# Moving the small transfers of a blocked inverse from SP's queue to ACT's in a hybrid decoder layer

## The chip, the cores and the metric

The kernel runs on one core of a Trainium2 chip. A core has a matrix engine (TensorE, here PE, with its weight loads shown apart as PEld), a vector engine (VectorE, DVE), a scalar engine (ScalarE, ACT), a general engine (GpSimd, POOL) and a queue engine (SyncE, SP). Each works through its own instructions in order and meets the others at semaphores. DMAs are issued from the queues of SP, ACT and POOL. The matrix engine writes to PSUM, the other operands lie in SBUF, and what doesn't fit goes through DRAM.

The metric is the device time of one execution in microseconds, as a median over runs.

## The reference

One layer of a decoder trunk on x of shape (1, 1024, 2048), all in float32, followed by an RMSNorm:

```python
h = rmsnorm(x, ln_g)
proj = h @ w_in                       # 2048 -> 6672 columns, split among three groups
out_a = gmlp_spatial_gating(...) * silu(g_z)          # 4 groups x 128, chunks of 128
out_b = rmsnorm(gated_delta_rule(q, k, v, g, beta)) * silu(d_z)   # 8 heads of 128
out_c = softmax(cq @ mk.T / sqrt(128)) @ mv * silu(c_z)           # 4 heads, 256 memory tokens
y = rmsnorm(x + concat(out_a, out_b, out_c) @ w_out, final_g)
```

The part that the change touches is in the gated delta rule. For each head and chunk it needs the inverse of a unit lower triangular matrix:

```python
a = where(strict, (k * beta) @ k.T * decay, 0)
T = triangular_solve(a + eye, eye, lower=True, unit_diagonal=True)
value, k_cumdecay = T @ (v * beta), T @ (k * beta * exp(g_cum))
```

## The kernel before

**Products.** Each large float32 product is made of three passes over operands split into a rounded high part and a rest (`split_to`, `triple`): ACT casts the high part, DVE subtracts for the low one, PE runs high-high, high-low and low-high. The first half of the heads is projected directly, in two halves of 512 tokens. The other projections and the output projection go through a scheme of seven products for eight (`seven`, `blocks`), whose sums of blocks are formed on DVE and kept in DRAM (`s_d`). A product's result gathers in one of four PSUM banks `acc`; the smaller products of the heads use four banks `dn`.

**The delta rule.** The kernel works on chunks of 128 tokens and on two heads at a time (a pair), in halves of 512 tokens: four chunks x two heads give eight 128 x 128 triangles per pair and half, in one tile `gt`. `front` makes q, k and `gt`. The inverse of a triangle is built from its four 32 x 32 diagonal blocks:

- `blocks_out` (line 967) stores the diagonal blocks to DRAM tensors `gdr`, one DMA for each of the four block positions. A DMA moves rows of 32 numbers (128 bytes).
- `inverse` (980) loads them so that every block lies in one partition (32 partitions per `gdr`, 1024 numbers in each; four loads per `gdr`), and runs 31 steps of two DVE instructions on all blocks at once, with a copy that transposes at the end. Two stores per `gdr` put the inverted blocks and their transposes into DRAM tensors `tdr` and `udr`.
- `levels` (1008) loads them back into block positions of the tiles `tblk` and `ut` (twelve loads and one transfer within `gt`), joins blocks of 32 to 64 and of 64 to 128 with small float32 products, and ACT copies the results out of PSUM.
- `scan_step` (1079) then carries the heads' states through the four chunks.

The first two pairs are inverted one at a time, for each half: four calls of `inverse`, on one `gdr` each. The last two pairs of both halves are gathered (`gdrs`) and inverted by one call on four `gdr` tensors, named "late", whose results are used by four later `levels` calls.

**The order of the work.** No instruction is placed by hand. Every call goes through `Engine` to `Plan.add`, which records it with its dependences. `Plan.price` gives it an estimated duration, and `Plan.issue` replays the whole program with these estimates: each engine takes, among what is ready, the lowest rank (`rank(...)`, 5 if none is given) and then the oldest. The order found is what each engine gets; at run time only semaphores hold an instruction back, so an engine waits at the first instruction whose data isn't there.

In that replay a DMA costs its issuing queue 380 ns on SP, 100 ns on ACT and 800 ns on POOL, less the engine's overlap (`OVERLAP`: none on SP, on ACT 90 ns but at most half the cost). The bytes of all DMAs push one cursor, `dma`, at 300 bytes per ns; a transfer lands 1600 ns after its end on the cursor, plus 3000 ns for a store to DRAM or 2400 ns for a load of small pieces. A product on PE costs 13.3 ns plus its columns at 2.4 per ns times its passes, at least 110 ns, and 30 ns if it doesn't fill 128 partitions.

`V`, `S`, `G`, `PE` and `Q` in the code are DVE, ACT, POOL, PE and the queue of SP. Nearly all DMAs are issued from `Q`: weights, block sums, spills and the inverse's transfers share it. Beside it ACT issues five small loads at the start and four stores at the very end. All instructions go out from line 277 (`o.fn(*o.args, **o.kw)` in `Plan.issue`), so the profile shows that line for everything, and tiles tell the groups apart.

Of the kernel before, what the change touches and what calls it, by code (L numbers as in the profile page):

```python
# [17 lines left out]
P = 128  # L18
# [44 lines left out]
class Plan:  # L63
# [21 lines left out]
    @contextmanager  # L85
    def rank(self, cls):
        old, self.cls = self.cls, cls
        yield
        self.cls = old
# [91 lines left out]
    def price(self, o, name, outs, ins):  # L181

        out = outs[0]
        n = math.prod(out.shape[1:])
        both = [*outs, *ins]
        psum = any(i.space == PSUM for i in both)
        pointer = any(i.shape[-1] == 1 and math.prod(i.shape[1:]) == 1 for i in ins[1:])
        o.nbytes = o.lock = 0
        o.lat = 0.0
        if name == "dma_start":  # L190
            o.cost = {"sp": 380.0, "act": 100.0, "pool": 800.0}[o.eng]
            rows = math.prod(out.shape[:-1])
            o.nbytes = max(4 * math.prod(out.shape), 512 * rows)
            src = ins[0]
            pieces = src.shape[-1] < 128 or out.shape[-1] < 128
            if out.space == DRAM:
                o.lat = 3000.0
            elif pieces or out.shape[0] < 32:
                o.lat = 2400.0
            elif list(src.ap)[0][0] == 0:  # L200
                o.lat = 4000.0
        elif o.eng == "pe":
            passes = 1 if ins[0].dtype == F32R else 2 if name == "transpose" else 4
            o.cost = max(13.3 + n / 2.4 * passes, 110.0) if out.shape[0] == P else 30.0
            o.lat = 175.0
        elif o.eng == "act":
            o.cost = (165.0 if psum else 200.0) + 0.82 * n + (105.0 if pointer else 0.0)
            o.cost += 190.0 if "accum_out" in o.kw else 0.0
        elif o.eng == "dve":
            n = max([n] + [math.prod(i.shape[1:]) for i in ins])  # L210
            o.cost = (n + 151) / 0.96 + (60.0 if pointer and name == "scalar_tensor_tensor" else 0.0)
            o.lock = not psum and (name.startswith("tensor_") or name == "scalar_tensor_tensor")
            o.lock = o.lock and name != "tensor_reduce"
        else:
            o.lock = 1
            if name in ("memset", "affine_select"):
                o.cost = 100.0 + 0.83 * n * (1 if name == "memset" else 1.4)
                o.lat = 800.0 if name == "affine_select" else 0.0
            else:
                o.cost = 750.0 + 150.0 * (n - 1) if n < 8 else 200.0 + 2.1 * n  # L220

    def issue(self):
        free = dict.fromkeys(self.SEEN, 0.0)
        soon = {e: [] for e in free}
        now = {e: [] for e in free}
        held = {"dve": 0.0, "pool": 0.0}
        dma = 0.0
        for o in self.ops:
            if o.n == 0 and o.lead is o:
                heapq.heappush(soon[o.eng], (0.0, o.idx))  # L230
        left = len(self.ops)
        while left:
            best = None
            for e in free:
                if now[e]:
                    t = free[e]
                elif soon[e]:
                    t = max(free[e], soon[e][0][0])
                else:
                    continue  # L240
                if best is None or t < best[0]:
                    best = (t, e)
            t, e = best
            while soon[e] and soon[e][0][0] <= t:
                i = heapq.heappop(soon[e])[1]
                heapq.heappush(now[e], (self.ops[i].cls, i))
            head = self.ops[heapq.heappop(now[e])[1]]
            for o in (head, *head.tail):
                t = max(t, free[e])
                o.at = t  # L250
                left -= 1
                if o.lock:
                    t = max(t, held["pool" if e == "dve" else "dve"])
                end = t + o.cost
                if o.lock:
                    held[e] = end
                free[e] = end - min(self.OVERLAP[e], 0.5 * o.cost)
                done = end + o.lat
                if o.nbytes:
                    dma = max(dma, end) + o.nbytes / self.DMA_RATE  # L260
                    done = dma + self.DMA_FIXED + o.lat
                for s in o.succ:
                    if s.eng != e or o.nbytes:
                        when = done + self.SEEN[s.eng] + (self.SLACK if s.eng == "pe" else 0.0)
                    elif e == "pe":
                        when = free[e]
                    else:
                        when = end + 34.0
                    s.ready = max(s.ready, when)
                    s.n -= 1  # L270
                    if s.n == 0:
                        heapq.heappush(soon[s.eng], (s.ready, s.idx))
            if len(head.tail) > 7:
                free[e] += self.SWITCH
        self.ops.sort(key=lambda o: (o.at, o.idx))
        for o in self.ops:
            o.fn(*o.args, **o.kw)  # L277
# [3 lines left out]
def kernel(  # L281
# [21 lines left out]
    x, mem, w_in, out = x[0], mem[0], w_in[0], out[0]  # L303
# [7 lines left out]
    V, S, G, PE, Q = R.dve, R.act, R.pool, R.pe, R.sp  # L311
# [5 lines left out]
    def DT(shape, name, dt=F32):  # L317
        return dr.tile(list(shape), dt, name=name, tag=name)[:]
# [35 lines left out]
    def bc(ap, n):  # L354
        return ap.unsqueeze(ap.ndim).to_broadcast(list(ap.shape) + [n])

    def rep(ap, n):
        return ap.unsqueeze(1).to_broadcast([ap.shape[0], n, ap.shape[1]])
# [211 lines left out]
    for k in range(KT):  # L570
# [11 lines left out]
        for h in range(NX):  # L582
            sl = slice(h * P, (h + 1) * P)
            triple(ka[h][:, :NMEM], (hi[:, sl], lo[:, sl]), (mh[:, kk], ml[:, kk]), k == 0, k == KT - 1)
        for mt in range(2):
            sl = slice(mt * P, (mt + 1) * P)
# [104 lines left out]
    for g in range(NG):  # L691
        sl = slice(g * P, (g + 1) * P)
# [274 lines left out]
    def blocks_out(gt, n):  # L967

        gv = gt.rearrange("p h t i -> p (h t) i")
        gdr = [DT([8, 32, 32], f"gdr{n}_{b}") for b in range(4)]  # L970
        for b in range(4):
            sl = slice(b * 32, (b + 1) * 32)
            with rank(1):
                Q.dma_start(gdr[b].rearrange("c j i -> j c i"), gv[sl, :, sl])
        return gdr

    def flat(start, *aps):
        start(*(a.rearrange("p a b -> p (a b)") for a in aps))

    def inverse(gdrs, n, cls):  # L980

        nr = 32 * len(gdrs)
        gd = ring["inv"]()[0:nr].rearrange("p (a b) -> p a b", b=32)
        for i, gdr in enumerate(gdrs):
            for b in range(4):
                with rank(1):
                    flat(Q.dma_start, gd[i * 32 + b * 8 : i * 32 + (b + 1) * 8], gdr[b])
        ti = ring["inv"]()[0:nr].rearrange("p (a b) -> p a b", b=32)
        tmp = (y1 if nr == 32 else y2)[0:nr].rearrange("p c m -> p (c m)")
        with rank(4):  # L990
            G.memset(ti, 0.0)
            G.affine_select(out=ti, in_=ti, compare_op=ALU.not_equal, fill=1.0, base=0,
                            pattern=[[1, 32], [-1, 32]], channel_multiplier=0)
        with rank(cls):
            for j in range(31):
                n1, m = 31 - j, j + 1
                tv = tmp[:, 0 : n1 * m].rearrange("p (n m) -> p n m", m=m)
                V.tensor_tensor(out=tv, in0=bc(gd[:, j, j + 1 :], m), in1=rep(ti[:, j, 0:m], n1), op=ALU.mult)
                V.tensor_tensor(out=ti[:, j + 1 :, 0:m], in0=ti[:, j + 1 :, 0:m], in1=tv, op=ALU.add)
            V.tensor_copy(gd.rearrange("p i m -> p m i"), ti)  # L1000
        tdr, udr = ([DT([32, 32, 32], f"{t}{n}_{i}") for i in range(len(gdrs))] for t in ("tdr", "udr"))
        for i in range(len(gdrs)):
            with rank(1):
                flat(Q.dma_start, tdr[i], ti[i * 32 : (i + 1) * 32])
                flat(Q.dma_start, udr[i], gd[i * 32 : (i + 1) * 32])
        return list(zip(tdr, udr))

    def levels(gt, tdr, udr):
# [179 lines left out]
    def inverted(n, *states):  # L1188
        return [(*s[:-1], i) for s, i in zip(states, inverse([s[-1] for s in states], n, 3))]
# [324 lines left out]
    with rank(2.6):  # L1514
        late_inv = inverse(gdrs, "late", 1.9)
# [265 lines left out]
```

## Time and profile before

| | before |
|---|---|
| median of 3 runs | 1648.26 us (1644.93 to 1648.33) |
| the profiled execution | 1647.33 us |
| its span, first to last instruction | 1645.6 us |
| mean granted clock of PE | 0.997 |
| busy PE / PEld | 1615.4 / 1354.1 us |
| busy DVE / ACT / POOL | 1323.4 / 1025.8 / 117.1 us |
| share of the span with DMA engines busy, SP's queue | 77.7% |
| bytes moved | 419.51 MB, 255 GB/s |

A busy time is the time in which the engine had an instruction at work. Issuing a DMA isn't counted as busy; the timeline shows it apart, with a q behind the engine's name (SPq, ACTq). Matmuls are pipelined and overlap in the records: a 128 x 512 product lasts 390 to 395 ns there, while the next one starts 0.23 us after it. An idle time in brackets stands in front of the instruction that ended it, with the engine or transfer that was waited for. A name such as `inv<-gdr` is the output tile and the input, without buffer numbers: here the loads of `inverse`. A float32 product that isn't split leaves two records on PE.

The profile shows the inverse's transfers as `gdr<-gt` (stores of `blocks_out`), `inv<-gdr`, `tdr<-inv` and `udr<-inv` (and `tdrlate`, `udrlate` for the late group), then `tblk<-tdr` and `ut<-udr` in `levels`.

### The profile page before, as it was taken

What the parts mean: (1) busy time and instruction counts of PE and PEld (TensorE: products, weight loads), DVE (VectorE), ACT (ScalarE), POOL (GpSimd) and SP (SyncE); (2) the same over time, 40 slices, a digit from 0 to 9 for tenths busy, and PEclk for the clock granted to TensorE, in tenths of its full rate; (3) what the DMA queues carried; (4) which work ended last, traced back from release to release, by engine and by line L of the source; (5) the groups of instructions that cost most, each with busy time, mean ns of one, the idle gap of its engine ahead of it and who ended that gap; (6) DMA issues with size and microseconds to landing.
All of it is one profiled execution on the core that took longest, in us unless ns stands there. A gap on an engine that the chain in (4) does not pass through costs nothing.

```text
span 1645.6 us, 26195 instructions
## 1 busy us (share of the span) xinstructions
PE 1615.4 (98%) x8570; PEld 1354.1 (82%) x8570; DVE 1323.4 (80%) x2288; ACT 1025.8 (62%) x2235; POOL 117.1 (7%) x139
## 2 busy tenths in 40 slices
PE   8999999899999999999999999999999999999997
PEld 6888887788888888888888787888888888888886
DVE  4866796767879869899999898879678898688875
ACT  6957764576846446877686546766657774344445
POOL 0001110210200000100101101000000000000001
PEclk9999999999999999999999999999999999999999
DMA  8989888586887877579877887889778789678646
GB/s 265 257 233 278 261 275 258 178 247 200 265 287 238 265 236 231 183 266 331 303 229 243 293 277 208 276 281 303 249 240 279 258 281 352 200 269 300 220 143 241
DMA packets 316659, 419.51 MB, mean 255 GB/s; under 512 B 57773, under 2 KB 138342, under 8 KB 316522
## 3 DMA queue, kind: packets, MB, share of 16 engines
q1 hardware_dynamic: 314818, 414.67, 77.7%
q0 software_dynamic: 1088, 2.10, 0.5%
q8 instruction: 67, 1.10, 0.3%
q10 hardware_dynamic: 616, 1.07, 0.2%
q14 instruction: 70, 0.57, 0.1%
HBM read 334.33 MB, written 82.87 MB: 254 GB/s over the span
## 4 chain that ended last, share of the span: by engine, by line
PE 88%; DVE 4%; DMA 4%; issue 1%; ACT 1%; POOL 1%; SPq 0%; POOLq 0%; DVEq 0%; ACTq 0%
PE acc L277 67%; PE dn L277 21%; DMA wraw<-in_w_in_dram 1%; DVE alo L277 1%; DVE wlo L277 1%; DVE y L277 1%; DMA wraw<-hTd 1%; POOL hs L277 1%; DMA E<-gcd 0%; DMA sd<-zg 0%; ACT whi L277 0%; DVE kT L277 0%; DMA y<-in_w_in_dram 0%; SPq L277 0%; DMA el<-vd 0%
## 5 line engine op out<-in xcount | busy, mean ns | idle before, releaser
L277 PE MATMUL acc<-ahi,whi 128*128 128x512 f32 (+1 forms) x1152 | 453.0, 394 | 7.3 <-ACT xr L277 4.5
L277 PE MATMUL acc<-ahi,wlo 128*128 128x512 f32 (+1 forms) x1152 | 451.1, 392 | 0.4 <-DVE small L277 0.4
L277 PE MATMUL acc<-alo,whi 128*128 128x512 f32 (+1 forms) x1152 | 450.6, 391 | 0.0
L277 PEld LDWEIGHTS acc<-ahi,whi 128*128 128x128 f32 x1152 | 217.3, 189 | 49.7 <-ACT xr L277 5.2
L277 PEld LDWEIGHTS acc<-ahi,wlo 128*128 128x128 f32 x1152 | 217.3, 189 | 41.7 <-DVE small L277 0.6
L277 PEld LDWEIGHTS acc<-alo,whi 128*128 128x128 f32 x1152 | 217.4, 189 | 40.7
L277 PE MATMUL acc<-ahi,zh 128*128 128x512 f32 x736 | 234.6, 395 | 0.9 <-DVE gt L277 0.9
L277 ACT CAST whi<-wraw 128x512 fp32r<-128x512 f32 (+1 forms) x170 | 137.1, 808 | 105.6 <-PE acc L277 67.1
L277 DVE TENSOR_TENSOR alo<-raws,ahi 128x1024 fp32r<-128x1024 f32 x131 | 159.9, 1221 | 38.6 <-ACT ahi L277 37.3
L277 ACT CAST ahi<-raws 128x1024 fp32r<-128x1024 f32 x131 | 137.4, 1049 | 69.1 <-PE dn L277 28.2
L277 DVE TENSOR_TENSOR wlo<-wraw,whi 128x1024 fp32r<-128x1024 f32 (+1 forms) x138 | 134.4, 975 | 49.1 <-ACT whi L277 43.1
L277 PEld LDWEIGHTS acc<-ahi,zh 128*128 128x128 f32 x736 | 137.2, 188 | 27.9 <-DVE gt L277 1.1
L277 PE MATMUL acc<-ahi,zl 128*128 128x512 f32 x368 | 145.1, 394 | 0.0
L277 DVE TENSOR_TENSOR ahi<-y,ahi 128x1024 fp32r<-128x1024 f32 x65 | 79.3, 1220 | 20.5 <-ACT ahi L277 20.2
L277 ACT CAST ahi<-y 128x1024 fp32r<-128x1024 f32 x65 | 68.2, 1049 | 39.4 <-PE acc L277 21.8
L277 PEld LDWEIGHTS acc<-ahi,zl 128*128 128x128 f32 x368 | 69.3, 188 | 13.1
L277 POOL TENSOR_TENSOR hs<-hs,mhalf 128x4 f32<-128x4 f32 x32 | 54.7, 1711 | 229.8 <-DVE hs L277 223.3
L277 ACT CAST zh<-wraw 128x1024 fp32r<-128x1024 f32 x36 | 37.8, 1051 | 44.4 <-PE acc L277 27.6
L277 POOL TENSOR_TENSOR small<-small,mhalf 128x1 f32<-128x1 f32 x26 | 19.6, 757 | 577.1 <-DVE small L277 577.1
L277 PE MATMUL dn<-whi,alo 128*128 128x512 f32 x152 | 59.1, 390 | 0.0
L277 PE MATMUL dn<-wlo,ahi 128*128 128x512 f32 x152 | 59.0, 389 | 0.0
L277 PE MATMUL dn<-whi,ahi 128*128 128x512 f32 x152 | 58.9, 390 | 0.0
(397 smaller groups left out, 3201.5 us busy)
## 6 DMA issues: line engine op xcount, KB each, us to landing
wraw<-in_w_in_dram SPq DMA_DIRECT2D x268, 256.0 KB
raws<-sd SPq DMA_DIRECT2D x148, 256.0 KB
y<-in_w_in_dram SPq DMA_DIRECT2D x92, 256.0 KB
y<-sd SPq DMA_DIRECT2D x77, 256.0 KB
wraw<-in_w_out_dram SPq DMA_DIRECT2D x64, 256.0 KB
raws<-h0d SPq DMA_DIRECT2D x54, 256.0 KB
y<-in_w_out_dram SPq DMA_DIRECT2D x33, 256.0 KB
low<-wlo SPq DMA_DIRECT2D x32, 256.0 KB
```

Source lines behind the costliest of these rows:

```text
L277: o.fn(*o.args, **o.kw)
```

## The change

Three things change. The stores of `blocks_out`, the loads of `inverse` and the stores at its end are issued from ACT's queue (`S`) and no more from SP's (`Q`). The loads of `levels` stay on SP. In the replay, a DMA of ACT has a cursor of its own, `beside`, on which its bytes count double, and it doesn't push the cursor of the other DMAs. And the estimate of an unsplit float32 product (four passes) that fills 128 partitions is at least 222 ns, where 110 was the floor for all.

```diff
@@ Plan.price
         elif o.eng == "pe":
             passes = 1 if ins[0].dtype == F32R else 2 if name == "transpose" else 4
-            o.cost = max(13.3 + n / 2.4 * passes, 110.0) if out.shape[0] == P else 30.0
+            o.cost = max(13.3 + n / 2.4 * passes, 222.0 if passes == 4 else 110.0) if out.shape[0] == P else 30.0
             o.lat = 175.0
@@ Plan.issue
-        dma = 0.0
+        dma = beside = 0.0
...
                 done = end + o.lat
-                if o.nbytes:
+                if o.nbytes and e == "act":
+                    beside = max(beside, end) + 2 * o.nbytes / self.DMA_RATE
+                    done = beside + self.DMA_FIXED + o.lat
+                elif o.nbytes:
                     dma = max(dma, end) + o.nbytes / self.DMA_RATE
                     done = dma + self.DMA_FIXED + o.lat
@@ blocks_out
-                Q.dma_start(gdr[b].rearrange("c j i -> j c i"), gv[sl, :, sl])
+                S.dma_start(gdr[b].rearrange("c j i -> j c i"), gv[sl, :, sl])
@@ inverse
-                    flat(Q.dma_start, gd[i * 32 + b * 8 : i * 32 + (b + 1) * 8], gdr[b])
+                    flat(S.dma_start, gd[i * 32 + b * 8 : i * 32 + (b + 1) * 8], gdr[b])
...
-                flat(Q.dma_start, tdr[i], ti[i * 32 : (i + 1) * 32])
-                flat(Q.dma_start, udr[i], gd[i * 32 : (i + 1) * 32])
+                flat(S.dma_start, tdr[i], ti[i * 32 : (i + 1) * 32])
+                flat(S.dma_start, udr[i], gd[i * 32 : (i + 1) * 32])
```

The lines that move stand under `rank(1)`, the lowest rank in use here, as before. Among 128 x 128 and wider products the new floor changes nothing (13.3 + 128 / 2.4 x 4 is already 226.6); it acts on the products of 64 columns in `levels` and on two of 32 columns in each `decays`.

## The prediction

> **What bounds the kernel now.** I read the page's engine totals first, then the busy time by stage, then every idle stretch of PE, then the transfers that move. The totals:
>
> ```profile
> span 1645.6 us, 26195 instructions
> PE 1615.4 (98%) x8570; PEld 1354.1 (82%) x8570; DVE 1323.4 (80%) x2288; ACT 1025.8 (62%) x2235; POOL 117.1 (7%) x139
> ```
>
> PE is busy for 1615.4 of 1645.6 us. No schedule can take more than the 30.2 us left, and no product is added or removed. The table by stage shows where those are (columns: stage, its width, busy time of PE, PEld, DVE, ACT, POOL, granted clock, DMA share, GB/s):
>
> ```profile
> 0.00:100.00 100.00, 92.54 (x569) 79.48 (x570) 65.78 (x124) 72.07 (x148) 6.45 (x18) 1.00 0.87 265
> 100.00:185.00 85.00, 85.00 (x431) 71.49 (x430) 58.50 (x112) 60.70 (x159) 11.04 (x15) 1.00 0.85 252
> 185.00:320.00 135.00, 129.96 (x715) 108.36 (x713) 106.36 (x268) 79.14 (x230) 14.03 (x10) 0.99 0.80 248
> 320.00:480.00 160.00, 156.63 (x960) 132.07 (x958) 120.02 (x255) 109.03 (x299) 26.60 (x24) 1.00 0.76 242
> 480.00:620.00 140.00, 140.00 (x751) 117.46 (x750) 110.43 (x185) 71.05 (x133) 3.23 (x5) 1.00 0.76 242
> 620.00:920.00 300.00, 295.71 (x1394) 245.67 (x1393) 277.66 (x441) 219.13 (x474) 29.57 (x33) 1.00 0.77 256
> 1020.00:1180.00 160.00, 158.31 (x1091) 135.91 (x1091) 129.79 (x200) 106.15 (x246) 8.68 (x14) 1.00 0.84 274
> ```
>
> The first 100 us come before any moved transfer. Between 185 and 1180 us PE idles 5.04 + 3.37 + 4.29 + 1.69 = 14.4 us; the rest is the start and the final drain. So the stage that holds the inverses has 14.4 us to win. The timeline of PE names the stretches; these rows carry most of them (in brackets the idle time and what ended it):
>
> ```profile
> 253.33 0.51 PE L277 MATMUL acc<-ahi,whi 128*128 128x512 f32 x1 [1.73 <-ACT xr L277]
> 312.72 0.80 PE L277 MATMUL acc<-ahi,whi 128*128 128x512 f32 x1 [2.81 <-ACT xr L277]
> 315.87 0.49 PE L277 MATMUL acc<-alo,whi 128*128 128x512 f32 x1
> 316.43 0.40 PE L277 MATMUL acc<-ahi,whi 128*128 128x512 f32 x1
> 316.66 0.40 PE L277 MATMUL acc<-alo,whi 128*128 128x512 f32 x1
> 324.15 1.21 PE L277 MATMUL dn<-ident,vs 128*128 128x128 f32 x4 [1.64 <-ACT vs L277]
> 381.69 0.49 PE L277 MATMUL dn<-states,kT 128*128 128x128 f32 x2 [0.82 <-ACT vs L277]
> 906.35 0.44 PE L277 MATMUL dn<-ident,gt 128*128 128x128 f32 x2 [1.39 <-ACT E L277]
> 1022.95 1.16 PE L277 MATMUL dn<-wsT,el 128*128 128x128 f32 x8 [1.69 <-DMA el<-vd]
> ```
>
> Five of these six end with a late ACT, one with a late transfer. None ends directly with an inverse's transfer. After the stall at 312.72 PE is also slow: from 312.72 to 315.87 seven products take 3.15 us from start to start, 0.45 each, where two of the same kind a little later (316.43 and 316.66) start 0.23 apart. That is about 1.5 us more, with the mean granted clock of that stage at 0.99.
>
> **The change, part by part.**
>
> *What moves.* Eighty DMA issues go from SP's queue to ACT's: 32 stores in `blocks_out`, 32 loads in `inverse`, 16 stores at its end. The transfers themselves, the loads of `levels` and all arithmetic stay. Each costs its queue this (minimum, median, maximum, ns):
>
> ```profile
> L277 SPq DMA_DIRECT2D gdr<-gt x32: 303/448/2274, 187.1 to 907.0; - x32
> L277 SPq DMA_DIRECT2D inv<-gdr x32: 263/293/588, 195.2 to 913.1; - x32
> L277 SPq DMA_DIRECT2D tdr<-inv x4: 318/408/442, 263.5 to 566.5; - x4
> L277 SPq DMA_DIRECT2D udr<-inv x4: 318/438/511, 264.6 to 569.7; - x4
> 995.11 2.73 SPq L277 DMA_DIRECT2D tdrlate<-inv  x4
> 997.94 1.77 SPq L277 DMA_DIRECT2D udrlate<-inv  x4
> ```
>
> 32 x 0.448 + 32 x 0.293 + 4 x 0.408 + 4 x 0.438 + 2.73 + 1.77 = 31.6 us of issuing leave SP. SP isn't the bound; its relief counts only where PE waits behind it.
>
> The Trainium skill, DMA: Bandwidth & Descriptors, section Issuing engines are not separate DMA queues, speaks against the change: DMAs run on the same engines whoever issues them, and issuing from several saves only the issuing time, usually small beside the transfer. By that rule the two gains that I find next would be nothing, and the sum below -1.2 instead of -3.7 us.
>
> *The late group's stores.* That is so once:
>
> ```profile
> 1000.72 2.85 SPq L277 DMA_DIRECT2D tblk<-tdrlate  x6
> 1003.61 8.16 SPq L277 DMA_DIRECT2D ut<-udrlate  x12
> 1011.87 0.38 SPq L277 DMA_DIRECT2D vd<-E  x1
> 1017.85 0.43 SPq L277 DMA_DIRECT2D el<-vd  x1
> ```
>
> From 995.11 to 999.71 SP issues eight inverse stores, then eighteen loads of `levels`, and only at 1011.87 the store whose reload ends the 1.69 us stall. Without the stores the eighteen loads can start up to 4.5 us sooner, as their source lands. I take the whole 1.69 us; the ends are 0 (the loads still wait for the landing) and 1.69. Behind it nothing else is late: the next product follows in that row's group.
>
> *The inverse loads of the third early pair.*
>
> ```profile
> 361.57 4.52 SPq L277 DMA_DIRECT2D gdr<-gt  x4
> 373.27 2.16 SPq L277 DMA_DIRECT2D inv<-gdr  x3
> 376.02 0.34 SPq L277 DMA_DIRECT2D wlo<-low  x1
> 376.61 0.26 SPq L277 DMA_DIRECT2D inv<-gdr  x1
> 380.91 0.18 DVE L277 TENSOR_TENSOR y<-inv,inv 32x31 f32<-32x31 f32 x1 [1.94 <-DMA inv<-gdr]
> ```
>
> The fourth load stands behind a weight load. DVE then stops 1.94 us for it with the state update queued behind, ACT's `vs` copy waits for that, and PE loses the 0.82 us at 381.69. Issued straight after the third (375.43) it would land 1.2 us sooner. That covers the 0.82; ends 0 and 0.82.
>
> *ACT's side.* The only ACT issues at steady work stand at the end:
>
> ```profile
> 1636.44 0.41 ACTq L277 DMA_DIRECT2D out_dram<-vs  x1
> 1637.05 0.46 ACTq L277 DMA_DIRECT2D out_dram<-y  x1
> ```
>
> So an issue on ACT costs about what it does on SP, and the first of a burst can run beside ACT's current instruction (1636.44 lies inside the activation of 1636.31 to 1637.01). ACT gets some 31.6 us on top of 1025.8, 3%, and is idle 620 us. The cover is that idle time. Without it a burst of four stores puts 4 x 0.448 = 1.8 us ahead of casts and PSUM copies. The loads' wait for the stores' landing now stands in ACT's queue; between the first store's and the first load's issue at 361.57 and 373.27 lie 11.7 us, so I count no wait there. The planner charges an ACT issue 100 ns less an overlap of 50, so it sees 4 us of the 31.6. The five stalls above that end with ACT sum to 8.4 us; 3% of that is 0.3 us, my term. The ends: 0, and 10 us if a third of the unplanned 27.6 us reaches PE (the rival below).
>
> *Estimates of small products.* Sixty-four products of `levels` go from 120 ns (13.3 + 64/2.4 x 4) to 222 in the plan, and four of `decays` from 110. The trace:
>
> ```profile
> 1015.86 1.00 PE L277 MATMUL dn<-tblk,gt 128*128 128x64 f32 x8
> 1016.67 0.71 PE L277 MATMUL acc<-ahi,zh 128*128 128x512 f32 x2
> ```
>
> Eight records are four fp32 products (two records each: the 64 products leave 128): 0.81 us, 202 ns each. The plan was 0.33 us short per group, 0.66 per `levels`, and will be 0.16 long. Stalls within some 40 us behind a `levels` call and not counted yet are 2.81 + 1.64 us and the 1.5 of slow clock, 6.0 us. I take a quarter, 1.5 us, as an estimate; ends are the whole 6.0 gained and, since the planner draws every order after the first `decays` anew, as much lost.
>
> *The model's DMA cursor.* ACT's transfers no longer push the cursor of SP's loads, and count double on their own. That changes order alone; it is in the ends just given.
>
> *Sum.* -1.69 - 0.82 + 0.3 - 1.5 = -3.7 us. The profiled execution took 1647.33 us (1.7 outside the span): 1643.6. The median of the runs, 1648.26, lies 0.9 above it, so 1644.5 beside the median. A measurement here tells 0.2%, 3.3 us, from no change; the forecast lies just beyond.
>
> **The rivals.**
>
> *ACT becomes the late one (slower).* ACT runs in order, so a store waiting for `gt`, or 1.8 us of issuing, delays the casts and copies behind it. Worst places are the four gdr stores at 361.57, 4.52 us in SP, while ACT would be copying for `levels`; and the eight stores at 995, where ACT empties PSUM:
>
> ```profile
> 996.12 0.58 ACT L277 COPY y<-acc 128x512 f32<-128x512 f32 x1
> 1000.19 0.58 ACT L277 COPY y<-acc 128x512 f32<-128x512 f32 x1
> ```
>
> Those four copies free the banks of the next product. For it: five of six stalls already end with ACT, and the plan is blind to 27.6 us. Against: ACT was idle 38%, and its casts mostly wait for PE to free a buffer (total us, times, longest):
>
> ```profile
> ACT whi L277 <- PE acc L277: 112.9, 90, 5.2
> ```
>
> If a third reaches PE, +9.2 - 2.5 = +6.7: 1655.0. With some nineteen bursts, it decides once 0.2 us of each sticks out (3.7/19), and it is slower by over 0.2% from 0.37 us.
>
> *The new order is worse (slower).* The present order has 14.4 us of stalls; one more like that at 312.72 with its slow clock, 4.3 us, and another like 253.33, 1.73, without the planned gains: 1654.3.
>
> *It is hidden anyway.* No PE gap ends with an inverse's transfer, and the two I count vanish into others, with the estimates' term at half and ACT's cost set against it: 1647.33 + 0.9 + 0.3 - 0.7 = 1647.8.
>
> This is where the rule of the Trainium skill quoted above (DMA: Bandwidth & Descriptors) leads. The trace so far bears it out in that SP's issuing is the one saving it shows.
>
> *More than I count (faster).* The gaps at 253.33, 312.72 with its clock, 324.15, 381.69 and 1022.95 all go: 1.73 + 4.3 + 1.64 + 0.82 + 1.69 = 10.2: 1638.1.
>
> **How the numbers follow.** Forecast 0.36, its own range 1640 to 1646; more gained 0.10; hidden 0.13; late ACT 0.27; worse order 0.14. The forecast's range crosses the bound of 0.2% at 1645.0, so 0.05 of it counts as same, and 0.02 of "hidden" as faster. Faster 0.31 + 0.10 + 0.02 = 0.43, same 0.05 + 0.11 = 0.16, slower 0.27 + 0.14 = 0.41. The range runs from just below the larger gain, 1637, to beyond the late ACT's 1655, 1658.
>
> **What would show it.** Right: the 80 issues stand under ACT's queue; the row at 1022.95 without its 1.69 us and DVE's wait for inv<-gdr gone; PE's idle time between 185 and 1180 at 11 us or less. Late ACT: ACT's time before casts and copies grows and PE's stalls ended by ACT come to more than 8.4 us. Worse order: stalls at new places whose waits name DVE or POOL, with ACT's issues standing in idle stretches. The prediction is wrong if ACT is held by one issue for 2 us (the longest on SP was 2274 ns) at a scan step, or if new stalls each bring the slow clock with them.

## The result, and the profile after

| | before | after |
|---|---|---|
| median of 6 runs each | 1648.96 us (1644.93 to 1655.01) | 1668.7 us (1666.13 to 1674.22) |
| ratio, with its 95% interval | 1 | 1.0118 (1.0092 to 1.0145) |
| the profiled execution, its span | 1647.33, 1645.6 us | 1666.31, 1664.6 us |
| mean granted clock of PE | 0.997 | 0.992 |

The change makes the kernel 1.2% slower. The forecast was 1644.5, the range 1637 to 1658: wrong in sign, and outside the range.

The engine totals of the changed kernel (all its instructions go out from line 280 now):

```profile
span 1664.6 us, 26198 instructions
PE 1623.0 (98%) x8570; PEld 1355.5 (81%) x8570; DVE 1317.2 (79%) x2288; ACT 1023.2 (61%) x2235; POOL 108.1 (6%) x139
```

The span is 19.0 us longer. PE's idle time grows from 30.2 to 41.6 us, its busy time from 1615.4 to 1623.0 with the same 8570 records. So PE stands still more, and is slower for a while. The busy time by stage (columns as in the prediction) says where:

```profile
185.00:320.00 135.00, 131.50 (x727) 109.14 (x726) 110.13 (x280) 83.74 (x249) 10.85 (x11) 1.00 0.81 242
320.00:480.00 160.00, 153.54 (x937) 128.71 (x936) 110.93 (x245) 102.41 (x287) 21.02 (x24) 0.98 0.76 229
480.00:620.00 140.00, 137.92 (x729) 114.88 (x728) 114.73 (x188) 75.11 (x140) 2.04 (x6) 0.99 0.77 254
620.00:920.00 300.00, 290.39 (x1348) 240.09 (x1347) 262.41 (x423) 207.29 (x448) 27.65 (x27) 0.98 0.77 254
920.00:1020.00 100.00, 96.04 (x519) 78.75 (x518) 88.28 (x155) 50.85 (x74) 8.52 (x12) 1.00 0.81 253
1020.00:1180.00 160.00, 160.00 (x1105) 137.52 (x1104) 129.19 (x208) 112.77 (x271) 13.14 (x17) 1.00 0.84 268
```

PE idles 25.6 us in these rows (before: 14.4), more than before in the four from 320 to 1020 us, and the clock falls to 0.98 in two of them. The timeline of PE has the stalls:

```profile
355.80 1.01 PE L280 MATMUL acc<-ident,tn 128*128 128x128 f32 x4 [1.83 <-ACT jk L280]
368.21 0.71 PE L280 MATMUL dn<-vs,ut 128*128 128x128 f32 x4 [2.62 <-ACT ut L280]
491.18 1.21 PE L280 MATMUL dn<-ident,vs 128*128 128x128 f32 x4 [2.08 <-ACT vs L280]
690.76 0.39 PE L280 MATMUL dn<-inv 128*128 128x256 f32 x1 [1.98 <-ACT inv L280]
894.51 0.48 PE L280 MATMUL dn<-ident,gt 128*128 128x128 f32 x1 [5.34 <-ACT gt L280]
898.04 0.48 PE L280 MATMUL dn<-ident,gt 128*128 128x128 f32 x1 [1.78 <-ACT gt L280]
1009.02 1.10 PE L280 MATMUL dn<-ut,y 128*128 128x64 f32 x8 [2.72 <-ACT y L280]
1016.68 1.06 PE L280 MATMUL dn<-wsT,el 128*128 128x128 f32 x8
```

All seven long ones end with ACT. The last row answers the 1.69 us stall of before at 1022.95: that product waits for nothing now. What ACT does ahead of the two stalls near 895 us stands in its own timeline (ACTq are the DMAs that it issues):

```profile
869.94 1.06 ACT L280 CAST ahi<-y 128x1024 fp32r<-128x1024 f32 x1
870.80 7.61 ACTq L280 DMA_DIRECT2D inv<-gdr  x12
878.46 0.40 ACT L280 ACTIVATE E<-E,hs 128x128 f32<-128x128 f32 x1 [7.46 <-DMA inv<-gdr]
...
884.69 3.49 ACTq L280 DMA_DIRECT2D gdr<-gt  x4
888.22 1.05 ACT L280 CAST whi<-wraw 128x1024 fp32r<-128x1024 f32 x1 [5.50 <-issue]
...
893.56 0.27 ACTq L280 DMA_DIRECT2D inv<-gdr  x1
893.87 0.59 ACT L280 COPY gt<-acc 128x512 f32<-128x512 f32 x1 [1.25 <-DMA wraw<-in_w_in_dram]
897.09 0.27 ACTq L280 DMA_DIRECT2D inv<-gdr  x1
897.40 0.59 ACT L280 COPY gt<-acc 128x512 f32<-128x512 f32 x1 [2.95 <-DMA raws<-sd]
```

The two copies of `gt` out of PSUM start as soon as the loads issued at 893.56 and 897.09 let them, and PE's products start 0.64 us after each copy's start. (The transfers in the brackets are those that landed last by the profile. Neither copy reads them; why ACT waits for them is the subject of a section below.) Before that the burst of twelve loads keeps ACT from any work for 7.46 us; twelve issues at their median of 281 ns are 3.4 of that, the rest is waiting between them. The waits of ACT name the inverse's transfers, which before's did not. Two of them:

```profile
ACT E L280 <- DMA inv<-gdr: 7.5, 1, 7.5
ACT kd L280 <- DMA gdr<-gt: 3.4, 1, 3.4
```

The other part of the loss is the clock. Busy time in windows of 2 us, the granted clock third from the end of each row:

```profile
890.00:892.00 2.00, 0.00 (x0) 0.00 (x0) 2.00 (x3) 2.00 (x5) 0.00 (x0) 0.96 0.45 81
892.00:894.00 2.00, 0.00 (x0) 0.00 (x0) 1.70 (x6) 0.75 (x2) 0.00 (x0) 0.50 0.97 337
900.00:902.00 2.00, 2.00 (x7) 1.48 (x6) 0.19 (x1) 1.26 (x2) 0.00 (x0) 0.50 0.94 315
902.00:904.00 2.00, 2.00 (x11) 1.60 (x10) 2.00 (x5) 1.21 (x2) 0.00 (x0) 0.98 0.31 87
```

From 892 to 902 us PE has half its clock, partly while it is idle. Adding (1 - clock) x busy time of PE over windows of 1 us from 100 to 1620 us gives 1.6 us before and 8.0 after. With the idle time between 100 and 1620 us (14.4 and 25.9 us) that is +6.4 and +11.5, 17.9 us of the 19.0 that the span is longer. The table below does the same for each run.

### The profile page after: what moved, and what is told of

Read it like the earlier page. It is cut to its first block, busy times and chain, and to the rows that moved or that the text cites. A ratio compares the mean times of both kernels' runs of the same rounds, so it can differ in the third digit from the quotient of the medians.

```text
span 1664.6 us, 26198 instructions
## 1 busy us (share of the span) xinstructions
PE 1623.0 (98%) x8570; PEld 1355.5 (81%) x8570; DVE 1317.2 (79%) x2288; ACT 1023.2 (61%) x2235; POOL 108.1 (6%) x139
## 4 chain that ended last, share of the span: by engine, by line
PE 72%; DMA 7%; DVE 5%; ACT 2%; issue 2%; ACTq 0%; SPq 0%; POOL 0%; POOLq 0%; DVEq 0%
PE acc L280 54%; PE dn L280 18%; DMA wraw<-in_w_in_dram 1%; DVE alo L280 1%; DMA E<-gcd 1%; DVE y L280 1%; DVE wlo L280 1%; DMA inv<-gdr 1%; DMA y<-in_w_in_dram 1%; ACTq L280 0%; ACT ahi L280 0%; DMA raws<-sd 0%; DVE ai L280 0%; DVE inv L280 0%; DMA zg<-hTd 0%
## 5 line engine op out<-in xcount | busy, mean ns | idle before, releaser
L280 POOL TENSOR_TENSOR hs<-hs,mhalf 128x4 f32<-128x4 f32 x32 | 48.4, 1516 | 204.4 <-DVE hs L280 203.4
L280 ACT CAST whi<-y 128x1024 fp32r<-128x1024 f32 x34 | 35.8, 1052 | 38.8 <-issue 20.4
```

## The experiments

My theory after this result, A: ACT, which works in order, is held by the DMAs in its own stream. The rival, B: the order that the planner draws anew is worse, wherever the DMAs stand. A recorded DMA can be sent from another queue than the planner thinks (its `fn` is replaced after recording), so the order and the queue can be changed one without the other.

| run | order | the eighty DMAs | ratio to before (95%) | PE idle, 100 to 1620 us | lost to half clock, us | span |
|---|---|---|---|---|---|---|
| before | old | SP | 1 | 14.4 | 1.6 | 1645.6 |
| after | new | ACT | 1.0118 (1.0092 to 1.0145) | 25.9 | 8.0 | 1664.6 |
| e1 | 222 ns alone | SP | 1.0033 (1.0016 to 1.0051) | 17.5 | 7.5 | 1654.1 |
| e2 | without 222 ns | ACT | 1.0117 (1.0094 to 1.0140) | 25.8 | 7.7 | 1666.9 |
| e3 | new | SP | 1.0057 (1.0038 to 1.0077) | 19.5 | 6.2 | 1655.4 |
| e4 | old | ACT | 1.0107 (1.0085 to 1.0128) | 25.0 | 6.7 | 1665.9 |
| e5 | old | stores ACT, loads SP | 1.0041 (1.0024 to 1.0059) | 19.7 | 1.5 | 1655.7 |
| e6 | old | loads ACT, stores SP | 1.0040 (1.0023 to 1.0056) | 17.0 | 4.6 | 1650.5 |
| e7 | old | POOL | 0.9991 (0.9976 to 1.0006) | 10.5 | 1.7 | 1643.6 |
| e8 | ACT's DMAs at 650 ns | ACT | 1.0238 (1.0207 to 1.0269) | 36.2 | 14.2 | 1686.7 |
| e9 | old | SP, and 80 spare on ACT | 1.0104 (1.0086 to 1.0122) | 26.5 | 9.2 | 1668.2 |
| e9b | old | SP, and 80 spare on POOL | 1.0007 (0.9993 to 1.0020) | 11.9 | 3.0 | 1648.6 |
| e12 | old | SP, and 160 spare copies on ACT | 1.0027 (1.0011 to 1.0043) | 18.5 | 6.4 | 1655.7 |
| e13 | old | SP, and 80 spare copies on ACT | 1.0021 (1.0005 to 1.0038) | 13.6 | 4.8 | 1650.3 |
| e10 | floor 130 ns | SP | 1.0043 (1.0028 to 1.0059) | 14.3 | 2.6 | 1657.5 |
| e14 | floor 160 ns | SP | 1.0139 (1.0118 to 1.0159) | 19.7 | 3.4 | 1668.6 |
| e11 | planned for POOL | POOL | 1.0018 (1.0003 to 1.0033) | 15.2 | 5.2 | 1651.2 |

The three columns on the right are of one profiled execution each; the idle time is 1520 us less PE's busy time there. For e6 and e7 that execution is a quick one (1652.21 us beside a median of 1657.3, and 1645.28 beside 1649.26), so their columns look better than the ratio.

### Order and queue apart (e1 to e4)

e1 is before with the new floor alone:

```diff
-            o.cost = max(13.3 + n / 2.4 * passes, 110.0) if out.shape[0] == P else 30.0
+            o.cost = max(13.3 + n / 2.4 * passes, 222.0 if passes == 4 else 110.0) if out.shape[0] == P else 30.0
```

> Kernel before with the floor of 222 ns alone; no DMA moves. Theory A (ACT is held by its own DMA issues, which the plan hardly sees): the estimate has no part in the loss, so 0.997 to 1.003 of before, about 1649 us. Theory B (the order drawn anew is worse whatever queue the DMAs stand in): a good part of the 19 us shows here, 1.006 or more.

e2 is the changed kernel with that line as it was.

> Changed kernel with the floor back at 110 ns: the eighty DMAs on ACT and the second cursor alone. Theory A: 1.008 to 1.015 of before, about as slow as the whole change, with ACT again the end of PE's stalls. Theory B (the estimate's new order is at fault): under 1.005.

e3 is the changed kernel, planned as it is, with the eighty DMAs sent from SP; e4 is the kernel before, planned as it is, with them sent from ACT. The edit of e4 (the other four calls alike; in e3 `S` and `nc.sync`):

```diff
-                Q.dma_start(gdr[b].rearrange("c j i -> j c i"), gv[sl, :, sl])
+                Q.dma_start(gdr[b].rearrange("c j i -> j c i"), gv[sl, :, sl]).fn = nc.scalar.dma_start
```

> The changed kernel's order of instructions on every engine, but the eighty DMAs are issued from SP's queue. Theory A: PE's stalls behind ACT at 368, 491 and 890 to 900 us and the half-speed stretches behind them go, and the time returns to 0.997 to 1.004 of before. Theory B: the order stays as bad as it is, 1.008 or more, with the same stalls.

> The order of the kernel before on every engine, but the eighty DMAs are issued from ACT's queue, at the places that they had on SP relative to the rest of the program. Theory A: ACT is held as in the changed kernel, or more since nothing was planned round it: 1.008 to 1.02 of before. Theory B: near 1.000, 0.997 to 1.004, as the order is the old one.

The queue is the larger part. With the old order it costs 1.07%, 17.6 us, on its own (e4). The order costs too: 0.57%, 9.4 us, with every DMA on SP (e3), where theory A had at most 0.4%. Together they cost 1.18%, not the sum. One reason that the traces show is that both make the stretch near 370 to 380 us wait. PE's timeline there in e3,

```profile
371.08 0.79 PE L280 MATMUL dn<-states,kT 128*128 128x128 f32 x2 [4.69 <-DVE states L280]
```

and in e4,

```profile
381.22 1.22 PE L277 MATMUL dn<-states,kT 128*128 128x128 f32 x4 [4.15 <-ACT vs L277]
921.61 0.44 PE L277 MATMUL dn<-ident,gt 128*128 128x128 f32 x2 [3.87 <-ACT E L277]
```

where before had 0.82 and 1.39 us. And in e3 the changed kernel's pair of stalls near 895 us is gone: the same twelve loads, in the same order of the program, leave SP while ACT goes on. SP's rows in e3:

```profile
871.57 0.97 SPq L280 DMA_DIRECT2D inv<-gdr  x3
...
873.04 2.35 SPq L280 DMA_DIRECT2D inv<-gdr  x7
...
875.84 0.66 SPq L280 DMA_DIRECT2D inv<-gdr  x2
```

and ACT's beside them:

```profile
870.72 1.05 ACT L280 CAST ahi<-y 128x1024 fp32r<-128x1024 f32 x1
871.67 0.40 ACT L280 ACTIVATE E<-E,hs 128x128 f32<-128x128 f32 x1
```

The activation of `E` follows its cast at once, where the changed kernel has the 7.46 us. Not every stall behind ACT is the queue's, though. The one of 2.08 us at 491.18 in the changed kernel, which theory A expected to go, stays in e3 with all eighty on SP:

```profile
491.13 1.21 PE L280 MATMUL dn<-ident,vs 128*128 128x128 f32 x4 [2.11 <-ACT vs L280]
```

That one belongs to the order. The estimate alone (e1) is a loss, 0.33%, between the two theories, and without it (e2) the change is as slow as with it.

### Which of the DMAs (e5, e6)

In e5 only the 48 stores have their `fn` replaced, in e6 only the 32 loads.

> The old order; only the 48 stores (gdr, tdr, udr) are issued from ACT, the 32 loads inv<-gdr stay on SP. Theory I (what holds ACT is the time of issuing): the stores have the longer issues, so most of the loss, 1.006 to 1.011 of before. Theory W (what holds ACT is the loads' wait for the stores' landing, which then stands in ACT's queue): little, 0.998 to 1.003, with no long wait of ACT for inv<-gdr.

> The old order; only the 32 loads inv<-gdr are issued from ACT, the stores stay on SP. Theory I: 32 x 0.28 = 9 us of issuing that lie in ACT's 620 idle us, 1.000 to 1.003. Theory W: most of the loss of the old order on ACT, 1.006 to 1.011, and ACT idle for several us in front of a cast at the loads of about 372 to 381 us and about 902 to 910 us.

Both cost 0.4%: neither theory as I put it. The stores hold ACT as much as the loads, so it isn't only the loads' wait for the stores' landing; and the loads cost although their issuing is 9 us.

### What a DMA in ACT's stream waits for

The compiled program, listed with the semaphores that each instruction waits for, shows what I had not looked at. ACT's part of the changed kernel, around the twelve loads (shortened names):

```
ahi1<-y3 128x1024           [waits DMAHW2,DMAHW1]
inv_44<-gdr02_0 8x1024      [waits DMAHW4,PE]
inv_44<-gdr02_1 8x1024      [waits DMAHW7]
inv_44<-gdr02_2 8x1024      [waits DMAHW2]
inv_44<-gdr02_3 8x1024      [waits DMAHW3]
inv_44<-gdr03_0 8x1024      [waits DMAHW4]
...
inv_44<-gdr12_3 8x1024      [waits DMAHW3]
E0<-E0,hs3 128x128
```

In this program all DMAs that SP and ACT issue take one of eight completion semaphores (DMAHW0 to 7) in turn, in the order of the program, and each waits until the DMA that last held its own has landed. On SP such a wait delays DMAs alone. In ACT's stream it stands in front of casts and PSUM copies, whether the DMA's own data is ready or not: the stores that these loads read were issued by 809 us, 62 us earlier, and the fifth load waits for the first to land, as both hold DMAHW4. POOL's DMAs take turns at eight others (DMASW), which no DMA of SP or ACT uses.

The traces show these waits at work. The loads issued at 893.56 and 897.09, above, share their semaphores with a weight load and a load of block sums of SP's: just the `wraw<-in_w_in_dram` and `raws<-sd` that the brackets name. The stall of 4.15 us in e4 comes from another such wait. ACT's rows in front of it:

```profile
377.91 0.28 ACTq L277 DMA_DIRECT2D inv<-gdr  x1
378.29 0.62 ACT L277 CAST whi<-wraw 128x512 fp32r<-128x512 f32 x1 [4.57 <-DMA E<-gcd]
```

The load at 377.91 reads a store whose semaphore had its last update by 373.37. It waits for `E<-gcd`, which SP issued at 371.00, which the load doesn't need, and whose semaphore had its last update at 377.84. The updates of the semaphores are on record, so this can be told for each of the eighty. In front of them ACT stands idle for 34.5 us in the changed kernel: 24.9 us end with the last holder of the DMA's own semaphore, 9.2 with DVE, which makes what a store reads, and 0.4 with a store that a load reads. In e4 it is 32.6 us, 23.3 of them for the last holder and 7.5 for DVE, and the rest can't be told; in e5 and e6 the last holder is waited for 8.1 and 8.4 us, about the same for stores and loads. While it issues, ACT is idle for some 31 us more in the changed kernel and 21 in e4. How the 17.6 us of e4 divide between waiting and issuing, these runs don't tell.

### Eighty DMAs that nobody needs (e9, e9b)

So such a wait might be put into ACT's stream by itself. e9 keeps order and DMAs of before, and adds at each of the eighty one of 512 bytes:

```diff
+            nc.sync.dma_start(*a, **k)
+            nc.scalar.dma_start(dummy[i : i + 1, :], ln_g[0:1, 0:128])
```

> The kernel before, its order and its eighty DMAs on SP as they are; at each of them ACT issues one more DMA of 512 bytes that nothing needs and that needs nothing, at the place in ACT's stream where the old order on ACT had its DMAs. In the list of waits each of these waits for one thing: that the DMA which last used its completion semaphore, one of eight that SP's and ACT's DMAs take in turn, has landed. Theory L (ACT stands behind the landing of other DMAs): the loss of the old order on ACT comes back without any data moved, 1.006 to 1.012 of before, with ACT idle several us in front of a cast at a burst. Theory D (only the data's own waits, a store's source and a load's store, hold ACT): 0.999 to 1.004, as 80 x 0.3 = 24 us of issuing lie in ACT's idle time.

> The same eighty spare DMAs, issued from POOL, whose DMAs use eight other semaphores. Both theories: 0.998 to 1.003; anything above is the price of the extra transfers themselves and is to be taken off the run with ACT.

The time is the one that theory L gives. The spare DMAs cost 1.04% on ACT, as much as the eighty real ones in the same order (1.07%), and nothing that can be measured on POOL. So the loss needs none of the data to go through ACT's queue. But the trace doesn't show ACT waiting as the theory has it. ACT's rows of e9 at the burst,

```profile
904.02 4.48 ACTq L975 DMA_DIRECT2D dummy<-in_ln_g_dram  x7
908.54 1.05 ACT L277 CAST zh<-wraw 128x1024 fp32r<-128x1024 f32 x1 [4.96 <-DMA inv<-gdr]
```

and PE's behind it:

```profile
922.95 0.69 PE L277 MATMUL dn<-ident,gt 128*128 128x128 f32 x2 [5.17 <-ACT E L277]
```

Seven issues at the median of 536 ns are 3.8 of the 4.48 us, and each follows the one before by 0.04 us: ACT is held here by issuing and not by a wait. Over the whole run it stands idle in front of the spare DMAs for only 6.3 us, against the 32.6 of e4, and for some 22 us while it issues them. The other bad place of e9, two stalls of PE of 2.16 us each near 388 and 391 us, lies behind a store that SP issues, by DVE's row:

```profile
386.03 1.42 DVE L277 TENSOR_TENSOR zg<-zg,zg 128x512 f32<-128x512 f32 x2 [5.89 <-DMA sd<-zg]
```

where before waits 1.72 us. SP itself now waits for the spare DMAs, as they take turns at its eight semaphores:

```profile
SPq L277 <- DMA dummy<-in_ln_g_dram: 8.8, 5, 3.3
SPq L974 <- DMA dummy<-in_ln_g_dram: 4.5, 8, 1.7
```

### Time taken or time waited (e12, e13)

An issue of a spare DMA lasts 536 ns in the median, 43 us for all, so e9 could be the time that they take of ACT. e12 puts two small copies in the place of each (e13 one):

```diff
-            nc.scalar.dma_start(dummy[i : i + 1, :], ln_g[0:1, 0:128])
+            nc.scalar.copy(jk[:, c : c + P], ident)
+            nc.scalar.copy(jk[:, c2 : c2 + P], ident)
```

> The kernel before, with two copies of 128x128 on ACT (about 0.5 us together) that nothing needs, at each of the eighty places where the run with spare DMAs had one of 0.54 us. It takes ACT's time as those did but waits for no DMA. Theory O (occupied time of ACT is the cost): 1.007 to 1.012 of before, like the spare DMAs. Theory L (the wait for landings is): 1.000 to 1.004.

> The same with one copy of 128x128 at each place, about 0.27 us, as long as an issue of inv<-gdr on ACT. Theory O: half of the run with two copies, 1.003 to 1.006. Theory L: 0.999 to 1.002.

The costliest groups of e12 show that they take 36.9 us of ACT, close to the 43:

```profile
L974 ACT CAST jk<-ident 128x128 bf16<-128x128 f32 x160 | 36.9, 300 | 0.1
```

That costs 0.27%, which is theory L's range, and with one copy 0.21%, just above theory L's and below theory O's: about a quarter of what the DMAs cost. So ACT's time as such, as far as copies stand for it, is the smaller part. The other three quarters must come from what a spare DMA has and two copies haven't. The traces show three such things: ACT's 6.3 us of waits, SP's 13.3 us of waits for them, and longer holds (at the burst sixteen copies take 3.30 us, where ACT stands 4.96 us behind the seven DMAs, and PE's stall for `E` is 2.21 us instead of 5.17). These runs don't part the three. What they show is that eighty DMAs cost this much in ACT's stream and not in POOL's.

### POOL's queue, and an honest price (e7, e8)

e7 is e4 with `nc.gpsimd` for `nc.scalar`.

> The old order; the eighty DMAs are issued from POOL's queue, an engine that is busy 7% of the span. If the loss is that ACT's casts and PSUM copies stand behind the DMAs, it goes: 0.996 to 1.004 of before, and what the relief of SP is worth by itself shows (the stall of 1.69 us at el<-vd gone or not). If any second queue costs (two queues sharing the DMA engines), 1.006 or more with PE's stalls ended by DMAs.

The same eighty DMAs cost nothing there. The inverse's loads of e7, by tile (durations in ns, minimum, median, maximum, and who waited):

```profile
L277 POOL DMA_DIRECT2D inv<-gdr x32: 497/508/578, 191.3 to 909.6; - x32
  POOL inv L277: 12.8, 10
```

An issue is dearer than on ACT, and POOL waits 12.8 us for landings, but POOL has few others waiting behind it. PE's row at the stall of 1.69 us before:

```profile
1018.46 1.16 PE L277 MATMUL dn<-wsT,el 128*128 128x128 f32 x8 [0.77 <-DMA el<-vd]
```

It is halved, the stall of 381.69 is gone, and PE's idle time falls by 3.9 us in this quick execution. The ratio, 0.9991 with its interval across 1, doesn't tell that from nothing. Beside e9b it is the only kernel here that isn't shown to be slower, and none is faster. Nor does a second queue, ACT's, slow SP's issuing down: its other 1668 issues take 711 us before and 707 in e4, with a median of 384 ns in both.

e8 asks whether the plan could have dodged the loss: `"act": 100.0` becomes `650.0` in `price`.

> The changed kernel with ACT's price for a DMA in the plan at 650 ns, about what one of the burst of twelve took, instead of 100. If the plan's price is the fault, the plan puts other work in front of the bursts and PE's stalls behind ACT fall from 23 us to under 12: 1.000 to 1.006 of before. If the fault is a wait for landing that the plan places too early (it counts under 5 us), a price changes little: 1.008 to 1.015.

Neither: it is the slowest of all. With the higher price the plan put fifteen of the late group's sixteen loads in one run, and ACT's rows show it standing still behind them:

```profile
882.70 10.84 ACTq L280 DMA_DIRECT2D inv<-gdr  x15
893.58 2.05 ACT L280 COPY y<-acc 128x512 f32<-128x512 f32 x4 [15.60 <-DMA inv<-gdr]
```

PE stalls 10.91 us there. Fifteen loads at 306 ns are 4.6 of the 10.84 us: a price per issue doesn't describe a wait for landings. Why the plan drew them together wasn't tried.

### Orders drawn anew (e10, e14, e11)

e10 and e14 change the floor of before to 130 and 160 ns. e11 issues the eighty from `G`, so that the plan knows of it.

> The kernel before with the floor of the products' estimate at 130 ns in place of 110: an order drawn anew for no reason; no DMA moves. If redrawing by itself loses (the present order is one of the better draws): 1.002 to 1.006 of before, like the estimate of 222 alone. If the 222 was at fault: 0.998 to 1.002.

> The kernel before with the estimate's floor at 160 ns: a second order drawn anew for no reason. If redrawing by itself loses: 1.002 to 1.006 again. If the floor of 130 was an unlucky draw: 0.997 to 1.002.

> The kernel before with the eighty DMAs given to POOL in the plan too (which prices them at 800 ns there), floor at 110. If the relief of SP with no load on ACT is worth what the prediction gave it (2.5 us): 0.997 to 1.000. If the redrawn order sets the time: 1.002 to 1.006.

e11 falls between its two expectations, e14 beyond both. With e1 and e3 that makes five orders drawn anew with no DMA on ACT, and all are slower, by 0.18 to 1.39%. But it isn't always the same place. This floor also holds for products of one and two passes, and e10 loses at the very start,

```profile
0.00:100.00 100.00, 88.11 (x521) 75.23 (x522) 61.57 (x102) 67.18 (x133) 6.45 (x18) 0.95 0.82 250
```

as does e14 (PE busy for 89.04 us there, x513). They end their first 100 us 48 and 56 records behind the 569 of before, and from 100 to 1620 us e10 idles as little as before (14.3 us). So a new order isn't a loss in each stretch; where e3 loses most is the place near 370 to 380 us where the change loses too, and e1 loses there and at the reload of `vd`. PE's rows of e1:

```profile
377.11 1.30 PE L277 MATMUL dn<-states,kT 128*128 128x128 f32 x4 [4.33 <-ACT vs L277]
1025.35 2.08 PE L277 MATMUL dn<-wsT,el 128*128 128x128 f32 x8 [2.96 <-DMA el<-vd]
```

## Why the prediction was wrong

**The step that failed is ACT's term, +0.3 us** ("ACT's side"). Three of its sentences fall short. "An issue on ACT costs about what it does on SP" holds for the issue (281 ns for `inv<-gdr` on ACT in the median, 293 on SP), not for what precedes it: ACT waits 34.5 us in front of the eighty, as long as all eighty issues take (33.6). "The cover is that idle time": the 620 idle us don't lie where the bursts fall, or not enough of them, as PE's stalls behind ACT show; e12 shows that even 36.9 us of plain work, 3.6% of ACT's, cost 0.27%, 4.5 us, so a share of 3% of the present stalls was no measure. "So I count no wait there": a wait for landing stands before nearly every moved DMA, on a shared semaphore, and I had looked only at the store that a load reads. The term is 17.6 us (e4), against an upper end of 10; by the table some 5 of it are the half clock behind the stalls.

**The late ACT, the rival with 0.27**, is what happened: right in mechanism, and in "five of six stalls already end with ACT", wrong in size. It decides at 0.2 us for each of nineteen bursts; measured it is 17.6 / 19 = 0.9. Of the two worst places that it named, the eight stores near 995 (975 to 981 now) have no stall of PE over 0.5 us in the 20 us behind them. At the third early pair the four stores take ACT 3.24 us, right before the 1.83 at 355.80, and its loads stand before the 2.62 at 368.21. The worst place, from the twelve loads at 870.80 to 898, it didn't name.

**The late group's stores, -1.69**, went as said: the product behind `el<-vd` no longer waits. In e7, with SP relieved in the same way, 0.77 us stays, within the ends. **The third early pair's loads, -0.82**: DVE's wait for `inv<-gdr` falls from 1.9 to 0.2 us after the change, and the stall of 381.69 is gone in e7. In the changed kernel a longer stall of ACT's takes its place. Both gains together are at most what e7 shows, 0.24% at the far end of its interval.

The Trainium skill, DMA: Bandwidth & Descriptors, section Issuing engines are not separate DMA queues, would have left these two gains at nothing. e7's ratio can't be told from that. That section prices what a second issuing engine saves. What it can cost isn't in that price, and here the cost decides: the same DMAs cost 1.07% from ACT and nothing that can be measured from POOL.

**The estimate, -1.5**, has the wrong sign: e1 measures +0.33%, 5.4 us, inside the ends of 6.0 either way. The plan is truer for those products and the order that it draws is worse. **The worse order, the rival with 0.14 and 1654.3**, is the second cause: 1658.6 in e3, with stalls that name DVE (4.69 us at 371.08), as its sign said.

**The half clock** was counted as a loss in the rivals alone; the sum has it only as something to gain. It is 6.4 of the 19 us. The prediction's last part said that it would be wrong "if ACT is held by one issue for 2 us" or "if new stalls each bring the slow clock with them". The longest single issue is 1794 ns, so the first did not come true. The second did in the main: there are four stretches of half clock, behind five of the seven long stalls, and none behind those at 690.76 and 1009.02.

## What to carry to other kernels

A DMA issued from a computing engine puts into that engine's stream its issuing and all that it waits for: its source, the landing of what it reads, and the DMA that last used its semaphore. List these waits and name what stands behind them before calling the engine's idle time a cover; if a second queue is wanted, take the engine with the fewest waiting behind it, here POOL. Price a stall of PE of more than some 2 us with a likely stretch of half clock behind it (the counts are below), and take an order drawn anew, for whatever reason, as a term of its own (here 0.2 to 1.4% slower in five of five).

## What was not expected of the hardware

The length of a stall alone doesn't tell whether half clock follows. In the nine kernels that keep the old order, PE has the same stall of 2.81 or 2.82 us for ACT's `xr` near 313 to 318 us. Behind it the clock is halved in seven (before, e4, e6, e7, e9, e9b, e13), for a sum of 1 - clock of 1.7 us in five and 3.4 in e9b and e13, and not in two (e5, e12). Over all profiles the shortest stall with half clock behind it and no other stall near was 1.67 us (e3), the longest without 2.86 us (e3). Of the 25 stalls of 2.0 to 2.9 us between 100 and 1620 us in the seventeen profiles, 18 have half clock at them or within 4 us behind; of the 20 longer ones, all. The stretches are 3.4 us long or a multiple of that: summed over one, 1 - clock gives 1.7, 3.4, 5.1 or (in e8) 6.8 us. The Trainium skill, TensorE: Matmul & The Clock Gate, section HAM oscillation — how this bites in real kernels, warns of idle gaps above about 3.4 us; the traces disagree with that bound, since 1.83 us at 355.80 was enough.
